# A hybrid decoder layer in split float32r on one Trainium2 core: the lower parts of some stationary weight pieces are summed by accumulating DMAs

## The chip, the cores and the metric

One core of one Trainium2 chip runs the whole layer as one program. The metric is device time in microseconds (us), the time of one execution. Three runs of the kernel before took 771.6, 767.98 and 767.42 us; their median is 767.98 us.

## The reference, cut to what matters

The layer has 512 tokens and a width of 1024. Three groups of heads read one normed input through one projection `w_in`, and one projection `w_out` merges them; then comes a SwiGLU feed-forward network of inner width 2816. Both parts are residual.

```python
h = rmsnorm(x, norm_mix); proj = h @ w_in
y_mla = mla_group(...)     # causal attention, low-rank q and kv
y_hg  = hgrn2_group(...)   # gated linear recurrence, chunkwise
y_mem = mem_group(...)     # cross-attention into 256 memory tokens
mix = concat([rmsnorm(y_mla), y_hg, rmsnorm(y_mem)])
x = x + mix @ w_out
h2 = rmsnorm(x, norm_ffn)
x = x + (silu(h2 @ w_gate) * (h2 @ w_up)) @ w_down
```

## The kernel before, in words

**Split products.** TensorE multiplies in fp32r, a float32 of fewer bits. Each operand is therefore cut in two: an upper part `hi`, which is the value cast to fp32r, and a lower part `lo = value - hi`. `mm3` (line 496) issues three matmuls for each product: hi by hi, hi by lo, lo by hi. For a weight that is the stationary operand the third of the three is the only one that reads the weight's `lo`.

**Weight pieces.** `load` (line 474) brings up to 1024 columns of a weight from HBM into a tile `wr` (3 buffers) with one DMA on SyncE's queue. `piece` (line 481) makes from up to 512 of its columns a pair: `wh`, cast by ScalarE (5 buffers), and `wl`, subtracted by VectorE (4 buffers). `pieces` (line 489) does this for a whole `wr` and hands out blocks of 128 columns. It is called in three places: `feat` (line 578), for the 20 blocks of `w_in` that come through `load` (40 pieces of 512 columns); the first eight of twelve row blocks of `w_out` (line 1132, 16 pieces); and `down` (line 1270), for `w_down`, where a block of six 128-wide steps gives a piece of 512 and one of 256 columns (24 times), and a block of four one piece of 512 (8 times). These are 112 pieces. All other weights (`wide`, the low-rank weights, the last rows of `w_out`, and gate and up in `fast`, line 1218) call `piece` directly.

**The order of the work.** Nothing is issued as it is written. A `Recorder` notes every operation with its tiles, and `run` (line 239) plays a list scheduler over them. It takes operations by priority, prices each (`price`, line 187), gives some operations to another engine where that ends sooner (a Copy activation with a scale may go from ScalarE to VectorE), keeps account of tile buffers, and writes out one fixed order for each engine. The engines then go through their own orders, and only semaphores hold them. So what TensorE does while it would wait for a piece is decided in the plan, not on the chip.

**The stages**, with the times of the profiled execution: the start (0 to 30 us) loads x and the first weights, splits x as it arrives, runs two products of `w_in` in turn (the accumulators `mm`), and sums the squares of x (tiles `td`, added up by VectorE), which four small matmuls with a column of ones (`tr<-ones,td`) turn into the norm of x. Then follow the recurrence and the low-rank products (to 200 us), attention, memory attention and the first eight rows of `w_out` as filler for TensorE (to about 345 us), the passage to the feed-forward network (to 440 us), and the network itself. Its products with gate and up are done by `fast`, one level of a Strassen-like scheme, on 384 columns at a time; between its steps the plan sets the `down` products of the stripe before. The last eight `down` products stand alone at the end.

Of the kernel before, what the change touches and what calls it, by code (L numbers as in the profile page):

```python
# [9 lines left out]
F32R = mybir.dt.float32r  # L10
I32 = mybir.dt.int32
U8 = mybir.dt.uint8
AF = mybir.ActivationFunctionType
ALU = mybir.AluOpType
# [3 lines left out]
S = 512  # L18
# [27 lines left out]
class Recorder:  # L46
# [140 lines left out]
    def price(self, o, outs, ins):  # L187
        n = max(self._free(a) for a in outs)
        if o.name == "dma_start":
            return 475  # L190
        if o.eng == "tensor":
            if o.name == "transpose":
                return 109
            if ins[0].dtype == F32R:
                return n / 2.4 + 12.5 if n >= 256 else max(1.67 * n, 107)
            return 222 if n <= 2 else 62 if n <= 32 else 118 if n <= 64 else 218 if n <= 128 else 1.7 * n
        m = max([self._free(a) for a in ins] + [n])
        fast = self.inside(ins)
        if o.eng == "scalar":
            fn = o.args[2] if o.name == "activation" else None  # L200
            if fn is not None:
                o.table = self.TABLES.get(str(fn).split(".")[-1])
            return (92 if fast else 45) + 0.835 * m + (190 if "accum_out" in o.kw else 0) + (100 if hasattr(o.kw.get("scale"), "ap") else 0)
        if o.eng == "vector":
            if o.name == "reciprocal":
                return 70 + 6.6 * m
            if o.name == "tensor_copy":
                return 66 + (0.55 if fast else 1.045) * m
            if o.name == "tensor_scalar":
                return 66 + (0.62 if fast else 1.045) * m + 60 * any(hasattr(a, "ap") for a in o.args[2:])  # L210
            if o.name == "memset":
                return 60 + 0.5 * m
            if o.name == "scalar_tensor_tensor":
                return 68 + 1.15 * m
            return 68 + 1.045 * m
        if o.name == "memset":
            return 40 + m * 0.8
        if o.name == "tensor_scalar":
            return 244 + 0.84 * m
        return 170 + 2.17 * m  # L220
# [18 lines left out]
    def run(self):  # L239
# [19 lines left out]
        table, dma, done, out, port = None, 0.0, 0, [], 0.0  # L259
        busy = {e: 0.0 for e in engs}  # L260
        while done < len(ops):
            best = None
            for e in engs:
                be = None
                for o in cand[e]:
                    t = max(free[e], o.ready)
                    if o.alts[e][5]:
                        t = max(t, port)
                    ok = True
                    if o.new:  # L270
                        need = {}
                        for k in o.new:
                            tag = self.tiles[k][0]
                            j = need.get(tag, 0)
                            free_ = slots[tag]
                            skip = 0
                            for q in order[tag]:
                                if q == k or skip >= len(free_):
                                    break
                                if q not in o.new:  # L280
                                    skip += 1
                            if len(free_) <= skip + j:
                                ok = False
                                break
                            t = max(t, sorted(free_)[skip + j])
                            need[tag] = j + 1
                    if not ok:
                        continue
                    t = max(t, free[e])
                    if len(o.alts) > 1:  # L290
                        fin = t + o.alts[e][3] + o.alts[e][4]
                        late = False
                        for e2 in o.alts:
                            if e2 != e:
                                t2 = max(free[e2], o.ready)
                                if o.alts[e2][5]:
                                    t2 = max(t2, port)
                                if e2 == o.home or t2 + o.alts[e2][3] + o.alts[e2][4] < fin:
                                    back = sum(q.alts[e2][3] for q in cand[e2] if q.prio < o.prio and q.home == e2 and q.ready <= t2 + 200)
                                    if t2 + back + o.alts[e2][3] + o.alts[e2][4] < fin:  # L300
                                        late = True
                        if late:
                            continue
                    c = (t, o.prio)
                    if t <= free[e] + 1e-9:
                        c = (free[e], o.prio)
                    if be is None or c < be[0]:
                        be = (c, o)
                if be is not None and (best is None or be[0][0] < best[0][0]):
                    best = be  # L310
                    beste = e
            assert best is not None, [(e, [(c.name, c.n, c.new) for c in cand[e][:3]]) for e in engs]
            (t, _), o = best
            for e in o.alts:
                cand[e].remove(o)
            o.eng = beste
            o.name, o.args, o.kw, cost, _, both = o.alts[beste]
            if o.eng != "scalar":
                o.table = None
            if o.table is not None and o.table != table:  # L320
                cost += 1300
                table = o.table
            end = t + cost
            if both:
                port = end
            free[o.eng] = end
            busy[o.eng] += cost
            if o.dma:
                ap = o.kw["out"]
                nb = self._free(ap) * ap.ap[0][1] * 4  # L330
                dma = max(dma, t + 1100) + nb / 360.0
                end = dma + 1500
            for k in o.new:
                tag = self.tiles[k][0]
                slots[tag].remove(min(slots[tag]))
                order[tag].remove(k)
            for k in o.tiles:
                last[k] = max(last[k], end)
                self.tiles[k][2] -= 1
                if self.tiles[k][2] == 0:  # L340
                    slots[self.tiles[k][0]].append(last[k] + 100)
            for s in o.succs:
                q = ops[s]
                q.left -= 1
                q.ready = max(q.ready, end + self.LAT.get((o.eng, q.eng), 0))
                if not q.left:
                    for e in q.alts:
                        cand[e].append(q)
            out.append((t, o))
            o.t, o.end = t, end  # L350
            done += 1
# [42 lines left out]
def body(ctx, tc, t):  # L394
    nc = tc.nc
    PS = bass.MemoryType.PSUM
    rec = Recorder(tc)
    V, A, G, T, DMA = rec.vector, rec.scalar, rec.gpsimd, rec.tensor, rec.sync
# [19 lines left out]
    def sb(tag, shape=(P, S), dt=F32):  # L418
        return rec.tile("SB", shape, dt, tag, nm(tag), BUFS[tag])
# [18 lines left out]
    def f(ap):  # L438
        return ap.bitcast(F32)
# [26 lines left out]
    def split(src, hi, lo, scale=None):  # L466
# [3 lines left out]
        else:  # L470
            A.activation(hi, src, AF.Copy, scale=scale)
            V.scalar_tensor_tensor(lo, src, scale, f(hi), ALU.mult, ALU.subtract)

    def load(src, n=1024):

        raw = sb("wr", (P, 1024))
        with rec.first(0):
            DMA.dma_start(out=raw[:, :n], in_=src)
        return raw

    def piece(raw, a, b):

        hi = sb("wh", dt=F32R)
        lo = sb("wl", dt=F32R)
        with rec.first(0):
            split(raw[:, a:b], hi[:, :b - a], lo[:, :b - a])
        return hi, lo

    def pieces(raw, n=1024):

        p = []
        for a in range(0, n, S):
            p.append(piece(raw, a, min(n, a + S)))
        return lambda k: cut(p[k // 4], slice(None), slice((k % 4) * P, (k % 4 + 1) * P))

    def mm3(out, l, r, first, last):
# [54 lines left out]
    with rec.first(0):  # L551
# [4 lines left out]
        for k in range(KD):  # L556
            if k in EARLY:
                n, tag = EARLY[k]
# [8 lines left out]
            hi = sb("xh", dt=F32R)  # L567
            lo = sb("xl", dt=F32R)
# [260 lines left out]
    with rec.first(0):  # L829
        for k in range(4):  # L830
            r = sb("td", (P, 2, NM))
            DMA.dma_start(out=r, in_=t["memT"][:, k * S:(k + 1) * S].rearrange("p (a b) -> p a b", a=2))
            hi = sb("mx", (P, 2, NM), F32R)
            lo = sb("mx", (P, 2, NM), F32R)
# [57 lines left out]
    for h in range(4):  # L892
        o = ps_mm()
# [10 lines left out]
    for b in range(NB):  # L904
        o = ps_mm()[:, :256]
# [3 lines left out]
        o = o.rearrange("p (h d) -> p h d", h=4)  # L909
# [44 lines left out]
    for i in range(2):  # L954
        w = [piece(r, i * S, (i + 1) * S) for r in wukv]
        for b in range(NB):
            o = ps_mm()
# [75 lines left out]
    for h in range(4):  # L1033
# [7 lines left out]
        o, qs = rope_t(qh, h)  # L1041
# [3 lines left out]
        o, kh2 = rope_t(kh, h)  # L1045
# [3 lines left out]
        for g in range(2):  # L1049
            pb = []  # L1050
            for b in (2 * g, 2 * g + 1):
# [3 lines left out]
                o = ps_at()  # L1055
# [32 lines left out]
    for h in range(4):  # L1088
        o = ps_mm()
# [18 lines left out]
    for h in range(4):  # L1108
# [6 lines left out]
        for g in range(2):  # L1115
            pb = []
            for b in (2 * g, 2 * g + 1):
                bs = slice(b * P, (b + 1) * P)
                o = ps_at()
# [287 lines left out]
```

## Time and profile before

| | before |
|---|---|
| median of the runs | 767.98 us |
| the profiled execution's own time | 769.33 us |
| its span, first to last instruction | 767.3 us |
| TensorE busy | 734.7 us (96%) |
| VectorE busy | 615.1 us (80%) |
| ScalarE busy | 391.6 us (51%) |
| GpSimd busy | 148.7 us (19%) |
| mean granted TensorE clock | 0.982 |
| DMA, mean over the span | 90 GB/s, queue of SyncE 29.4% of 16 engines |

PE is TensorE's matmuls and PEld its weight loads, DVE is VectorE, ACT ScalarE, POOL GpSimd, and SP SyncE, which here only issues DMAs. In a row, out<-in are the tiles with their shapes, x a count, then busy time in us and the mean of one in ns, then the idle time just before and what ended it. All recorded operations have the same line (370), so rows are told apart by tile names. A matmul's time is from its start to its end in the pipeline; the distance between starts is what TensorE spends on it.

### The profile page before, as it was taken

Reading aid. Unit: us, or ns where it says so; the run is one execution under the profiler, and the core shown is the slowest. Engines: PE = TensorE matmul, PEld = TensorE weight load, DVE = VectorE, ACT = ScalarE, POOL = GpSimd, SP = SyncE. Lnnn points to the kernel's source line nnn. Section 1 sums busy time; section 2 is a strip of 40 time slices with the busy share of each in tenths; the row PEclk is TensorE's granted clock in tenths of the full one; section 3 lists DMA queues with packets and bytes.
Section 4 is the critical chain, followed back from the end, with each engine's and each line's share of the span. In section 5 each row is a group of like instructions: output and inputs, shape, how many; then the busy total and the mean of one; then the engine's idle time right before and its main releaser. Section 6 shows DMA issues by size and latency. Waiting matters only on the chain.

```text
span 767.3 us, 12180 instructions
## 1 busy us (share of the span) xinstructions
PE 734.7 (96%) x4117; PEld 646.9 (84%) x4117; DVE 615.1 (80%) x1415; ACT 391.6 (51%) x790; POOL 148.7 (19%) x166
## 2 busy tenths in 40 slices
PE   6999998999999999899898799999999999999997
PEld 4899887888788888788677699999989998999986
DVE  6887788765997888896899899778887788886762
ACT  6543335226674476565475465455354553555440
POOL 1133233114201021010330203210221101201101
PEclk9999999899999999999999899999999999999999
DMA  8231113012541132211423423251522513142132
GB/s 274 71 111 47 65 56 96 21 28 87 163 136 56 51 128 83 69 43 54 146 62 95 124 82 93 73 156 40 145 83 84 154 41 107 56 123 71 35 110 97
DMA packets 36206, 69.38 MB, mean 90 GB/s; under 512 B 4272, under 2 KB 21296, under 8 KB 36144
## 3 DMA queue, kind: packets, MB, share of 16 engines
q1 hardware_dynamic: 36144, 68.61, 29.4%
q8 instruction: 32, 0.52, 0.3%
q14 instruction: 30, 0.25, 0.1%
HBM read 66.50 MB, written 2.10 MB: 89 GB/s over the span
## 4 chain that ended last, share of the span: by engine, by line
PE 64%; DVE 7%; issue 1%; DMA 1%; ACT 1%; DVEq 0%; ACTq 0%
PE mm L370 30%; PE tr L370 18%; PE at L370 17%; DVE wl L370 2%; DVE y L370 1%; DVE tm L370 1%; DVE p L370 1%; DMA mx<-in_wu 1%; DVE tc L370 1%; DVE mx L370 1%; DVE xl L370 0%; DVE hd L370 0%; DVE xh L370 0%; DVE sm L370 0%; DVE td L370 0%
## 5 line engine op out<-in xcount | busy, mean ns | idle before, releaser
L370 ACT CAST wh<-wr 128x512 fp32r<-128x512 f32 (+2 forms) x151 | 86.2, 575 | 120.6 <-PE mm L370 81.8
L370 ACT CAST wh<-mx 128x384 fp32r<-128x384 f32 (+1 forms) x160 | 77.5, 486 | 91.4 <-PE at L370 40.7
L370 PE MATMUL mm<-xh,wh 128*128 128x512 f32 x244 | 99.3, 410 | 7.1 <-ACT xh L370 7.1
L370 DVE TENSOR_TENSOR wl<-wr,wh 128x512 fp32r<-128x512 f32 (+2 forms) x141 | 96.7, 693 | 10.5 <-issue 4.0
L370 PE MATMUL mm<-xl,wh 128*128 128x512 f32 x244 | 99.4, 407 | 2.5 <-DVE xl L370 2.5
L370 PE MATMUL mm<-xh,wl 128*128 128x512 f32 x244 | 98.8, 405 | 0.0
L370 DVE TENSOR_TENSOR wl<-mx,wh 128x384 fp32r<-128x384 f32 (+1 forms) x141 | 74.1, 536 | 14.1 <-PE at L370 5.8
L370 PE MATMUL mm<-wh,hd 128*128 128x384 f32 (+2 forms) x232 | 71.2, 331 | 2.7 <-ACT wh L370 1.7
L370 PEld LDWEIGHTS mm<-xh,wh 128*128 128x128 f32 x244 | 46.9, 193 | 16.7 <-ACT xh L370 8.5
L370 PEld LDWEIGHTS mm<-xl,wh 128*128 128x128 f32 x244 | 46.9, 192 | 12.9 <-DVE xl L370 5.2
L370 PE MATMUL at<-wh,hd 128*128 128x384 f32 (+1 forms) x176 | 56.4, 325 | 0.0
L370 PEld LDWEIGHTS mm<-xh,wl 128*128 128x128 f32 x244 | 46.8, 192 | 8.6 <-DVE wl L370 0.4
L370 PE MATMUL tr<-xh,wl 128*128 128x512 f32 x132 | 52.0, 394 | 0.5 <-DVE wl L370 0.5
L370 PE MATMUL tr<-xl,wh 128*128 128x512 f32 x132 | 51.9, 393 | 0.0
L370 PE MATMUL tr<-xh,wh 128*128 128x512 f32 x132 | 51.7, 392 | 0.0
L370 ACT CAST wh<-y 128x384 fp32r<-128x384 f32 (+1 forms) x64 | 30.9, 486 | 35.4 <-PE at L370 19.5
L370 PE MATMUL mm<-wh,v 128*128 128x384 f32 (+1 forms) x128 | 42.5, 336 | 5.9 <-ACT wh L370 5.4
L370 PEld LDWEIGHTS mm<-wh,hd 128*128 128x128 f32 x232 | 43.0, 189 | 5.5 <-ACT wh L370 2.0
L370 DVE TENSOR_TENSOR tm<-tr,tm 128x512 f32<-128x512 f32 x30 | 20.6, 687 | 31.9 <-PE tr L370 31.9
L370 POOL TENSOR_TENSOR wl<-mx,wh 128x384 fp32r<-128x384 f32 (+1 forms) x19 | 19.3, 1016 | 129.4 <-PE at L370 51.6
L370 PE MATMUL at<-wh,v 128*128 128x384 f32 (+1 forms) x128 | 41.8, 330 | 0.0
L370 POOL TENSOR_TENSOR wl<-wr,wh 128x512 fp32r<-128x512 f32 (+2 forms) x17 | 21.4, 1264 | 104.6 <-PE mm L370 55.6
(369 smaller groups left out, 1968.8 us busy)
## 6 DMA issues: line engine op xcount, KB each, us to landing
wr<-in_wf SPq DMA_DIRECT2D x20, 512.0 KB, 3.4
wr<-in_wd SPq DMA_DIRECT2D x24, 384.0 KB, 3.2
mx<-in_wg SPq DMA_DIRECT2D x24, 192.0 KB, 2.7
y<-in_wg SPq DMA_DIRECT2D x24, 192.0 KB, 2.4
mx<-in_wu SPq DMA_DIRECT2D x24, 192.0 KB, 2.5
y<-in_wu SPq DMA_DIRECT2D x24, 192.0 KB, 2.6
tm<-in_xT SPq DMA_DIRECT2D x16, 256.0 KB, 4.1
wr<-in_wt SPq DMA_DIRECT2D x8, 512.0 KB, 4.2
```

Of the source, the lines that this page charges most:

```text
L370: r = getattr(getattr(self.nc, o.eng), o.name)(*[get(a) for a in o.args], **{k: get(a) for k, a in o.kw.items()})
```

## The change

The 112 pieces that `pieces` makes get their `lo` in another way. ScalarE casts `hi` as before; a second activation writes `-hi` into `lo`; then a DMA issued by GpSimd reads the same weights from HBM once more and adds them to `lo` in place. `load` notes for each `wr` where it came from. The scheduler's prices get an entry for such a DMA: 1000 ns of GpSimd to issue it instead of 475, and a transfer at 180 GB/s instead of 360. These are the plan's assumptions, not measurements.

```diff
-            return 475
+            return 475 if o.eng == "sync" else 1000
...
-                dma = max(dma, t + 1100) + nb / 360.0
+                dma = max(dma, t + 1100) + nb / (360.0 if o.eng == "sync" else 180.0)
...
+    def piece_dma(raw, a, b):
+        hi = sb("wh", dt=F32R)
+        lo = sb("wl", dt=F32R)
+        with rec.first(0):
+            A.copy(hi[:, :b - a], raw[:, a:b])
+            A.activation(lo[:, :b - a], f(hi)[:, :b - a], AF.Copy, scale=-1.0)
+            G.dma_start(out=lo[:, :b - a], in_=home[raw.tensor.name][:, a:b], accum_op=ALU.add)
+        return hi, lo
...
-            p.append(piece(raw, a, min(n, a + S)))
+            p.append(piece_dma(raw, a, min(n, a + S)))
```

Since the plan is made anew, the orders of all engines change. VectorE goes from 1413 to 1361 rows: 81 of its 110 subtractions from `wr` of 512 columns and all 25 of 256 columns are gone, 13 of the negations are given to it, and it takes over other operations. ScalarE goes from 758 to 832 rows and has 99 of the negations. GpSimd has 112 DMAs more and 25 tensor operations fewer.

At the start, TensorE's order around the four small matmuls `tr<-ones,td`. The accumulators mm_2157 and mm_2201 are the first two products of `w_in` in both orders, mm_2299 (before) and mm_2266 (after) the third; wl_2199 is the lower part of the second product's first piece. Before:

```order
L370 MATMUL mm_2299<-xl_2184,wh_2260 128x512
L370 MATMUL mm_2299<-xh_2176,wl_2276 128x512
L370 MATMUL mm_2299<-xh_2203,wh_2260 128x512
L370 MATMUL mm_2299<-xl_2213,wh_2260 128x512
L370 MATMUL mm_2299<-xh_2203,wl_2276 128x512
L370 MATMUL mm_2299<-xh_2216,wh_2266 128x512
L370 MATMUL tr_2328<-ones,td_2306 128x2 x4
L370 MATMUL mm_2299<-xl_2229,wh_2266 128x512
L370 MATMUL mm_2299<-xh_2216,wl_2288 128x512
```

After:

```order
L370 MATMUL mm_2157<-xl_2238,wh_2210 128x512
L370 MATMUL mm_2157<-xh_2229,wl_2217 128x512
L370 MATMUL mm_2157<-xh_2236,wh_2210 128x512
L370 MATMUL mm_2157<-xl_2244,wh_2210 128x512
L370 MATMUL mm_2157<-xh_2236,wl_2217 128x512
L370 MATMUL mm_2266<-xh_2149,wh_2256 128x512
L370 MATMUL mm_2266<-xl_2155,wh_2256 128x512
L370 MATMUL tr_2288<-ones,td_2275 128x2 x4
L370 MATMUL mm_2201<-xh_2149,wl_2199 128x512
L370 MATMUL mm_2201<-xh_2161,wh_2189 128x512
L370 MATMUL mm_2201<-xl_2172,wh_2189 128x512
```

Before the change 61 matmuls of 512 columns stand ahead of the small ones, after it 28; the second product, but for two matmuls, has moved behind them.

In the feed-forward network, TensorE's order where the third `down` product of the first stripe begins; tr_7663 (before) and tr_7730 (after) are its accumulator, wl_7645 and wl_7685 the lower part of its first piece, and mm and at are those of `fast`. Before:

```order
L370 MATMUL at_7619<-wh_7598,pth_6698 128x384
L370 MATMUL tr_7663<-xh_7275,wh_7613 128x512
L370 MATMUL tr_7663<-xl_7292,wh_7613 128x512
L370 MATMUL tr_7663<-xh_7275,wl_7645 128x512
L370 MATMUL tr_7663<-xh_7282,wh_7613 128x512
```

After:

```order
L370 MATMUL at_7680<-wh_7657,pth_6752 128x384
L370 MATMUL tr_7730<-xh_7331,wh_7674 128x512
L370 MATMUL tr_7730<-xl_7348,wh_7674 128x512
L370 MATMUL mm_7737<-wh_7706,v_6344 128x384
L370 MATMUL mm_7737<-wl_7719,v_6344 128x384
L370 MATMUL mm_7737<-wh_7706,v_6580 128x384
L370 MATMUL at_7742<-wh_7706,v_6344 128x384
L370 MATMUL at_7742<-wl_7719,v_6344 128x384
L370 MATMUL at_7742<-wh_7706,v_6580 128x384
L370 MATMUL mm_7737<-wh_7717,v_6344 128x384
L370 MATMUL at_7742<-wh_7717,v_6344 128x384
L370 MATMUL tr_7730<-xh_7331,wl_7685 128x512
```

Eight matmuls of `fast` now stand between the first use of the piece's upper part and the first use of its lower part.

At the same place GpSimd's order, where wl is the lower part of a weight piece, of gate and up if it comes from mx or y. Before:

```order
L370 TENSOR_TENSOR mx_7157<-y_7228,mx_7157 128x384
L370 TENSOR_TENSOR wl_7558<-mx_7112,wh_7550 128x384
L370 TENSOR_TENSOR wl_7609<-mx_7157,wh_7598 128x384
L370 TENSOR_TENSOR mx_7578<-mx_7578,mx_7571 128x384
L370 TENSOR_TENSOR wl_7787<-y_7215,wh_7755 128x384
```

After:

```order
L370 TENSOR_TENSOR wl_7661<-mx_7159,wh_7645 128x384
L370 TENSOR_TENSOR wl_7668<-mx_7213,wh_7657 128x384
L370 DMA wl_7685<-in_wd 128x512
L370 DMA wl_7702<-in_wd 128x256
L370 TENSOR_TENSOR mx_7687<-mx_7687,mx_7672 128x384
L370 TENSOR_TENSOR wl_7780<-y_7284,wh_7752 128x384
```

Each `down` product now puts two DMAs between GpSimd's subtractions for `fast`, and what stands behind them waits until they are issued.

More of the change, by code (lines that the diff above doesn't have):

```diff
@@ L472, in split @@
             V.scalar_tensor_tensor(lo, src, scale, f(hi), ALU.mult, ALU.subtract)
+    home = {}
     def load(src, n=1024):
@@ L478, in load @@
             DMA.dma_start(out=raw[:, :n], in_=src)
+        home[raw.tensor.name] = src
         return raw
```

## The prediction, as put on record before the run

> **What bounds the kernel now.** I read the page's busy times first, then the windows by stage, then what TensorE waited for.
>
> ```profile
> span 767.3 us, 12180 instructions
> ...
> PE 734.7 (96%) x4117; PEld 646.9 (84%) x4117; DVE 615.1 (80%) x1415; ACT 391.6 (51%) x790; POOL 148.7 (19%) x166
> ```
>
> TensorE is idle for 32.6 us of the span. That bounds what relief of VectorE can bring, apart from the clock. The windows, one row for each stage (busy us, granted clock, DMA share, GB/s), show where these 32.6 us lie:
>
> ```profile
> core 0: us, PE busy (x) PEld busy (x) DVE busy (x) ACT busy (x) POOL busy (x), PEclk, DMA share, GB/s
> 0.00:30.00 30.00, 23.87 (x100) 17.50 (x101) 21.21 (x51) 18.49 (x31) 2.92 (x8) 1.00 0.63 203
> 30.00:128.00 98.00, 97.38 (x670) 86.77 (x669) 78.73 (x202) 41.33 (x79) 32.35 (x47) 1.00 0.22 72
> 128.00:200.00 72.00, 67.67 (x373) 56.68 (x372) 52.07 (x141) 30.93 (x62) 23.75 (x25) 0.93 0.19 59
> 200.00:345.00 145.00, 143.02 (x789) 120.53 (x788) 127.06 (x353) 89.84 (x183) 17.75 (x22) 0.99 0.29 90
> 345.00:440.00 95.00, 81.72 (x389) 69.88 (x388) 83.44 (x178) 53.27 (x110) 18.91 (x15) 0.93 0.33 96
> 440.00:740.00 300.00, 298.02 (x1705) 276.82 (x1704) 244.43 (x485) 154.67 (x325) 49.15 (x47) 1.00 0.31 89
> 740.00:767.00 27.00, 23.02 (x102) 18.75 (x100) 8.12 (x12) 3.07 (x5) 3.88 (x3) 1.00 0.34 115
> ```
>
> Idle: 6.1 us at the start (before the first x is there), 0.6, 4.3, 2.0, 13.3, 2.0, and 4.0 at the end. In the feed-forward network, 300 us long, TensorE has nothing to gain: 2 us. The stages at 128 and 345 us have waits and also a clock of 0.93, which costs some 5.0 and 6.7 us more (7% of each). What ended TensorE's waits:
>
> ```profile
> PE mm L370 <- ACT wh L370: 7.1, 2, 5.4
> PE mm L370 <- ACT xh L370: 7.1, 2, 6.1
> PE mm L370 <- DVE xl L370: 2.5, 1, 2.5
> PE at L370 <- POOL tm L370: 1.9, 1, 1.9
> ...
> PE mm L370 <- DVE wl L370: 1.2, 3, 0.5
> ```
>
> The subtraction that the change takes away, DVE wl, is waited for by three matmul groups for 1.2 us in all. TensorE bounds the kernel, and the subtraction is hidden beside it.
>
> **VectorE, ScalarE and GpSimd.** The costs of one, by shape:
>
> ```profile
> L370 DVE TENSOR_TENSOR wl<-wr,wh 128x512 fp32r<-128x512 f32 x110 | 83.1, 757 | 8.7 <-issue 3.6 <-PE mm L370 2.7 <-PE tr L370 1.0
> L370 DVE TENSOR_TENSOR wl<-mx,wh 128x384 fp32r<-128x384 f32 x105 | 58.4, 567 | 10.4 <-PE at L370 5.1 <-PE tr L370 2.4 <-ACT wh L370 2.3
> ...
> L370 DVE TENSOR_TENSOR wl<-wr,wh 128x256 fp32r<-128x256 f32 x25 | 11.5, 459 | 1.6 <-PE at L370 0.7 <-issue 0.3 <-PE mm L370 0.3
> ...
> L370 DVE CAST wh<-wr 128x512 fp32r<-128x512 f32 x6 | 2.5, 424 | 0.9 <-PE mm L370 0.9
> ```
>
> ```profile
> L370 ACT CAST wh<-wr 128x512 fp32r<-128x512 f32 x117 | 72.3, 621 | 100.8 <-PE mm L370 68.0 <-PE tr L370 20.1 <-PE at L370 3.7
> ```
>
> VectorE loses 81 x 0.757 + 25 x 0.459 = 72.8 us, gains 13 negations at about 0.42 (the cast is the nearest row) = 5.5, and some 41 other operations (1413 - 106 + 13 = 1320, and it has 1361) at about 0.55 = 23: from 615 to about 570 us. ScalarE gains 77 negations at about 0.62 (the cast again) and 22 of half the width at less, 48 to 61 us, and hands some work on: about 430. Both stay below TensorE, so none of this is in the sum by itself. It counts only where VectorE holds TensorE: at 128 to 200 and at 345 to 440 us. In the second the order has no piece of the changed kind, and VectorE's 83.4 us there are the residual, its norm and the feed-forward operands, which stay: 0 us, with the bound below. In the first, TensorE's wait for POOL tm and its slow clock can go, because the plan sets 3.6 us more of matmuls ahead of that chain's last ones: between 0 and 4.3 + 5.0 = 9.3 us; I take 3, near the one wait of 1.9 with some clock.
>
> **The start.** Sums of squares and second product, before:
>
> ```profile
> 17.78 0.68 DVE L370 TENSOR_TENSOR td<-td,td 128x512 f32<-128x512 f32 x1
> 18.39 0.68 DVE L370 TENSOR_TENSOR wl<-wr,wh 128x512 fp32r<-128x512 f32 x1
> ...
> 22.60 0.68 DVE L370 TENSOR_TENSOR td<-td,td 128x512 f32<-128x512 f32 x1
> ...
> 22.86 0.39 PE L370 MATMUL mm<-xl,wh 128*128 128x512 f32 x1
> 23.09 0.39 PE L370 MATMUL mm<-xh,wl 128*128 128x512 f32 x1
> ...
> 23.55 0.95 PE L370 MATMUL tr<-ones,td 128*128 128x2 f32 x8
> ```
>
> Matmuls start 0.23 us apart, and the small ones come at 23.55, when td is ready. In the new order 28 instead of 61 wide matmuls stand ahead of them: 33 x 0.23 = 7.6 us of work has moved behind a point that TensorE cannot pass before td is ready. td comes sooner, though: between 17.78 and 23.28 VectorE does five adds and four subtractions at 0.6 us each; after, one negation and one cast (0.42 each) and the 0.42 mask cast stand there with four adds: 3.7 instead of 5.5 us, 1.8 sooner. ScalarE must then do its part by 20.6, and by its rows it can. TensorE starts the rest 7.6 - 1.8 = 5.8 us poorer, and in the 98 us that follow it is idle for 0.6 us, so nothing there gives this back: +5.8 us. This does not hang on the DMA's speed, since wl_2199, whose upper part is cast at 11 us, has some 10 us to land. If td came no sooner it would be 7.6; if ScalarE and VectorE ran free of it, 4.
>
> **The accumulating DMAs.** The profile has none, nor any DMA issued by GpSimd. The nearest row (KB each, us from issue to landing):
>
> ```profile
> wr<-in_wo SPq DMA_DIRECT2D x8, 256.0 KB, 2.7
> ```
>
> Below, a piece of 256 KB lands in 2.7 us, if adding costs nothing. Above, in twice that, if old and new data pass one after the other, and 1.0 us of GpSimd to write it out (as long as one of its tensor operations, below): 6.4. I take 4.5: 2.7, another 256 KB at the 321 GB/s that the start reaches (0.8), and 1.0 to issue, the estimates' middle.
>
> ```profile
> 10.00:20.00 10.00, 9.92 (x40) 7.03 (x40) 9.76 (x15) 8.98 (x16) 2.15 (x1) 1.00 0.89 321
> ```
>
> ```profile
> L370 POOL TENSOR_TENSOR wl<-mx,wh 128x384 fp32r<-128x384 f32 x15 | 16.3, 1090 | 102.0 <-PE at L370 48.1 <-ACT wh L370 41.8 <-ACT xh L370 6.2
> ```
>
> The chain for one piece: TensorE frees the buffer, ScalarE negates (0.62), GpSimd issues, the sum lands, TensorE reads. From td's end to the small matmuls a hand-over took 23.55 - 23.28 = 0.27 us; two such, 0.5, since the landing's is in its time. That is 0.5 + 0.6 + 4.5 = 5.6 us, with ends 3.8 and 7.5. Against it stands the room in TensorE's own order, from the last use of the buffer's piece before to the first use of the new one. Up to 345 us it is 5.6 us at the least and mostly 9 to 16: hidden, and at 7.5 us it costs 4. In the feed-forward network it is short. For wl_7685, whose buffer held wl_7635, 27 matmuls of 384 columns and two of 512 stand between:
>
> ```profile
> 475.65 0.33 PE L370 MATMUL at<-wl,hd 128*128 128x384 f32 x1
> 475.83 0.33 PE L370 MATMUL at<-wh,hd 128*128 128x384 f32 x1
> 476.00 0.33 PE L370 MATMUL mm<-wh,v 128*128 128x384 f32 x1
> ```
>
> 27 x 0.174 + 2 x 0.23 = 5.2 us. Counted so, the first pieces of the 24 `down` products among `fast` have 4.8 to 6.3 us but for one, about 5.6 in the mean; the second pieces, and the last eight products, have over 6.3 but for one. At a chain of 5.6 us the shorter half waits, 12 pieces for 0.1 to 0.8 us, in the mean 0.37: +4.5 us. At 5.1 it is nothing; at 6, +10; at 7.5, 24 x 1.9 = 46. Behind the issuing GpSimd stand subtractions for `fast`, 1.1 us each, for which matmuls wait in turn; ahead of it, ScalarE's casts for `fast` stand behind the negation. Subtractions for `fast` have less room too, since two of four wl buffers are held by a `down`: the tightest tenth of them 1.4 us instead of 2.4, against 0.57 for the subtraction and 0.54 for two hand-overs. The cover left is 0.3 us: 0 in the sum, and 0.3 us and more for each where VectorE comes late by that much. DMA time itself is no bound: 26 MB more beside the 0.31 share here.
>
> The Trainium skill speaks to this price. Collectives: The Full Stack, Part 3 (the bandwidth ceiling), says that a reducing DMA is half as fast as a copy since it needs two source reads; DMA: Bandwidth & Descriptors, Anatomy of one DMA, gives 2.0 us and bytes / 436 GB/s for a DMA from GpSimd. Its estimate for a plain 256 KB is 2.6 us, to which the 2.7 measured on SyncE's queue agrees; with double bytes 3.2 us, a chain of 4.3 and no wait at all. By that the sum would be 4.5 us less; no run here shows it yet.
>
> **The sum**, on the profiled execution: 769.3 + 5.8 - 3 + 4.5 = 776.6. That execution is 1.35 us above the median of the runs; on the median 768.0 + 7.3 = 775.
>
> **The rivals.** About 0.5% (3.8 us) is what a measurement here can tell from no change.
> - *Late landing.* The sum takes 6 us or more from issue, or GpSimd needs well over 1 us to write it out; the network's 24 `down` products then stall one by one, and GpSimd's subtractions with them. For: their room is so even that they all tip together, at a chain of 5.6 us. Against: the rows of plain loads. Price: 768 + 2.8 + 10 to 46 = 781 to 817, and TensorE's clock, which is 0.93 where it waits, could add to it.
> - *Early landing.* The sum lands within 4 us: no wait in the network, and the start and the chain at 128 us alone remain: 768 + 2.8 = 771, within 0.5%. The two pages of the Trainium skill named above would have it so.
> - *Faster: VectorE runs ahead.* Where VectorE is 88 to 93% busy (200 to 440 us), 48 pieces fewer let its chain into the network start sooner against TensorE, and the 13.3 us of waits and 6.7 us of clock at 345 to 440 shrink by half; those at 128 us go wholly. 768 + 5.8 - 9.3 - 10 = 755. It decides if more than 10 us of these 29 go and the sums land in time. Against: in TensorE's order the norm before the network stands 1.3 us later than before, not earlier, and the work between is what it was.
> - *It doesn't do what it says.* The plan fills VectorE up again, and everything stays as it was, start included: 768.
>
> **How the numbers follow.** Forecast (775, from 772 to 781) 0.40; late 0.22; early 0.20; faster 0.14; nothing 0.04. Faster by over 0.5%: 0.14. Within: early and nothing, 0.24. Slower: forecast and late, 0.62. The range leaves out the faster half of the one and the dearer half of the other: from 762 (half the gain) to 801 (+30 in the network, a chain of 6.9 us).
>
> **What would show it.** Right: VectorE near 570 and ScalarE near 430 us; the small matmuls at 21.8 us and TensorE idle for some 6 us between 12 and 22; in the issues, wl<-in_wf with landings near 4.5 us; waits of TensorE for wl from a DMA of a few us in all, between 440 and 740 us. Wrong: a landing of 6 us or more; GpSimd's issue over 1 us; the stage at 345 us with 8 us of idle or less; or TensorE as busy at the start as before.

## The result, and the profile after

The changed kernel took 791.71 us (median of 4 runs, 789.81 to 797.01), the kernel before 767.7 us beside it: a ratio of 1.0315, 95% interval 1.0281 to 1.035. It is 24 us slower; 7 were forecast. The profiled execution took 789.81 us. Its page, with busy times and DMA queues:

```profile
span 788.0 us, 12426 instructions
...
PE 736.3 (93%) x4117; PEld 642.4 (82%) x4117; DVE 572.3 (73%) x1363; ACT 423.8 (54%) x865; POOL 218.2 (28%) x253
...
q1 hardware_dynamic: 36144, 68.61, 28.8%
q0 software_dynamic: 16128, 26.22, 21.1%
```

The change does what it says: VectorE fell by 43 us, ScalarE rose by 32, and a second queue moves 26 MB, whose packets take 21.1% of the 16 DMA engines, nearly twice as much per byte as SyncE's 28.8% for 68.6 MB. TensorE is busy for nearly as long as before (736 us, 735 before), but it is idle for 51.7 us instead of 32.6. The same stages as before:

```profile
0.00:30.00 30.00, 21.53 (x68) 14.29 (x69) 18.06 (x53) 19.64 (x32) 5.79 (x13) 0.94 0.86 242
30.00:128.00 98.00, 97.85 (x668) 87.74 (x667) 71.06 (x188) 43.32 (x85) 32.26 (x47) 1.00 0.49 114
128.00:200.00 72.00, 68.61 (x407) 57.34 (x406) 53.70 (x152) 35.28 (x72) 26.53 (x29) 1.00 0.28 74
200.00:345.00 145.00, 142.19 (x802) 120.60 (x801) 119.67 (x349) 99.02 (x205) 37.70 (x45) 1.00 0.62 142
345.00:440.00 95.00, 82.94 (x398) 70.87 (x397) 86.15 (x180) 54.76 (x108) 21.88 (x18) 0.95 0.40 107
440.00:740.00 300.00, 281.86 (x1579) 257.62 (x1578) 208.34 (x419) 155.51 (x335) 82.12 (x89) 1.00 0.47 113
740.00:788.00 48.00, 41.33 (x205) 33.90 (x203) 15.32 (x30) 16.28 (x32) 11.92 (x14) 0.98 0.67 149
```

Two rows stand out. At the start TensorE has 68 matmuls done in 30 us where it had 100. Between 440 and 740 us it is idle for 18 us where it was for 2. Of the four stages between 30 and 440 us the first has two matmuls fewer than before and the others have more, and the granted clock at 128 to 200 is 1.00 instead of 0.93. TensorE's waits, and then those of its weight loads, which take in what matmuls still in the pipeline hide:

```profile
PE tr L370 <- DMA wl<-in_wd: 16.1, 19, 2.4
PE mm L370 <- ACT wh L370: 7.1, 2, 5.0
PE mm L370 <- ACT xh L370: 6.2, 2, 5.5
PE tr L370 <- DVE td L370: 2.8, 2, 2.1
```

```profile
PEld tr L370 <- DMA wl<-in_wd: 22.3, 22, 2.8
```

The row of the sums is new: 22 times the weight load of a `down` product waits for its sum, 22.3 us in all, 1.0 us each.

Where on the way the time is lost shows best when the two traces are laid over each other by matmuls. The table gives how much later (+) or sooner (-) than in the kernel before the n-th matmul starts, counted from the first; it is worked out from the matmuls' start times in the traces. The orders differ, so the n-th matmul is not always the same product; both kernels have 4117. In the kernel before, matmul 1100 starts at about 190 us, 2000 at 358, 2400 at 455.

| n-th matmul | 100 | 1100 | 2000 | 2400 | last (4117) |
|---|---|---|---|---|---|
| changed kernel, us | +6.8 | +0.4 | -0.9 | -3.4 | +21.6 |

The start costs 6.8 us, the middle gives 10.2 back, and the network takes 25.0. Together that is 21.6 us where the medians differ by 24: the profiled execution is the fastest of the four, and that of the kernel before took 1.6 us more than its median.

### The profile page after: what moved, and what is told of

The parts are those of the page before. It is cut to its first block, busy times and chain, and to the rows that moved or that the text cites. A ratio compares the mean times of both kernels' runs of the same rounds, so it can differ in the third digit from the quotient of the medians.

```text
span 788.0 us, 12426 instructions
## 1 busy us (share of the span) xinstructions
PE 736.3 (93%) x4117; PEld 642.4 (82%) x4117; DVE 572.3 (73%) x1363; ACT 423.8 (54%) x865; POOL 218.2 (28%) x253
## 3 DMA queue, kind: packets, MB, share of 16 engines
q1 hardware_dynamic: 36144, 68.61, 28.8%
q0 software_dynamic: 16128, 26.22, 21.1%
## 4 chain that ended last, share of the span: by engine, by line
PE 44%; DMA 16%; DVE 6%; issue 4%; ACT 3%; POOL 1%; ACTq 0%; DVEq 0%; POOLq 0%
PE mm L370 19%; PE tr L370 16%; DMA wl<-in_wd 14%; PE at L370 9%; DVE wl L370 2%; ACT wl L370 1%; DVE mx L370 1%; ACT wh L370 1%; DMA wl<-in_wo 1%; DMA wl<-in_wf 1%; POOL wl L370 1%; DVE xl L370 1%; DMA mx<-in_wu 0%; DVE tc L370 0%; DVE tm L370 0%
## 5 line engine op out<-in xcount | busy, mean ns | idle before, releaser
L370 ACT CAST wh<-wr 128x512 fp32r<-128x512 f32 (+2 forms) x145 | 83.1, 577 | 113.6 <-PE mm L370 70.7
L370 ACT CAST wh<-mx 128x384 fp32r<-128x384 f32 (+1 forms) x155 | 75.0, 486 | 93.8 <-PE tr L370 46.3
L370 DVE TENSOR_TENSOR wl<-mx,wh 128x384 fp32r<-128x384 f32 (+1 forms) x131 | 70.2, 545 | 19.0 <-PE at L370 7.1
L370 POOL DMA_DIRECT2D wl<-in_wd x56 | 49.8, 950 | 73.9 <-ACT wl L370 56.3
L370 PE MATMUL tr<-xh,wl 128*128 128x512 f32 x132 | 53.9, 409 | 15.4 <-DMA wl<-in_wd 15.3
L370 ACT ACTIVATE wl<-wh 128x512 fp32r<-128x512 f32 (+1 forms) x99 | 56.8, 580 | 16.8 <-issue 5.7
L370 POOL DMA_DIRECT2D wl<-in_wf x40 | 35.2, 881 | 95.1 <-ACT wl L370 54.4
L370 POOL TENSOR_TENSOR wl<-mx,wh 128x384 fp32r<-128x384 f32 (+1 forms) x29 | 27.7, 956 | 110.6 <-PE tr L370 33.4
L370 PE MATMUL tr<-xh,wh 128*128 128x512 f32 x132 | 51.7, 391 | 0.0
```

What stands on the lines that cost most here:

```text
L370: r = getattr(getattr(self.nc, o.eng), o.name)(*[get(a) for a in o.args], **{k: get(a) for k, a in o.kw.items()})
```

## The experiments

The theory was that the loss is TensorE's wait for sums that land late in the network (the landing theory). Its rivals were a cost spread over all pieces (GpSimd's issue, ScalarE's negations, HBM traffic) and a shortage of wl buffers. Each row is one of the edits below; each ratio is to the kernel before on the same chip, with its 95% interval. Delays are as in the table above.

| kernel | median us | ratio | n=100 | 1100 | 2000 | 2400 | last |
|---|---|---|---|---|---|---|---|
| `down` subtracted | 766.99 | 1.0004 (0.9981 to 1.0028) | +6.3 | +0.9 | -0.5 | -2.9 | -2.9 |
| only `down` accumulated | 789.56 | 1.0301 (1.026 to 1.0341) | +1.5 | +1.4 | +1.4 | +0.3 | +20.9 |
| late plan | 772.85 | 1.0073 (1.0045 to 1.0101) | +7.0 | +0.2 | -3.2 | -7.7 | +4.3 |
| plain copy | 766.54 | 0.9979 (0.9955 to 1.0003) | +8.6 | +3.4 | -0.4 | -2.4 | +2.8 |
| five wl buffers | 786.39 | 1.0248 (1.0203 to 1.0293) | +6.6 | +1.6 | -1.1 | -4.2 | +17.3 |
| start subtracted | 783.41 | 1.0193 (1.0161 to 1.0226) | +0.8 | -4.5 | -6.4 | -8.4 | +16.6 |
| start and `down` subtracted, late plan | 757.17 | 0.9861 (0.9834 to 0.9888) | +1.3 | -2.5 | -5.9 | -10.2 | -10.3 |
| start subtracted, late plan | 767.36 | 1.0012 (0.9987 to 1.0038) | +0.5 | -2.2 | -5.5 | -9.6 | -1.0 |
| start and `down` subtracted | 759.73 | 0.991 (0.9878 to 0.9942) | +0.4 | -5.1 | -6.6 | -9.5 | -9.4 |
| start subtracted, late plan, five buffers | 767.4 | 1.0003 (0.9974 to 1.0032) | +1.2 | -2.9 | -4.5 | -9.3 | -1.9 |
| start and `down` subtracted, late plan, five buffers | 758.85 | 0.9897 (0.9846 to 0.9948) | +0.6 | -4.9 | -6.5 | -10.1 | -9.4 |

### Half of the pieces each

`pieces` takes the way of cutting as an argument; `down` hands in `piece`, the others keep `piece_dma`.

```diff
-            p.append(piece_dma(raw, a, min(n, a + S)))
+            p.append((cut_ or piece_dma)(raw, a, min(n, a + S)))
...
-        w = pieces(load(t["wd"][i][:, j0 * P:(j0 + n) * P], n * P), n * P)
+        w = pieces(load(t["wd"][i][:, j0 * P:(j0 + n) * P], n * P), n * P, piece)
```

> The 56 pieces of the down products are subtracted by VectorE again; the 56 others keep the accumulating DMAs. Landing theory (the loss is the wait of TensorE for late sums in the feed-forward network): the 25 us lost after 440 us go, and what stands at 440 us stays, 3 us ahead of the kernel before: 763 to 767 us. Rival (GpSimd's issue time, ScalarE's negations and the added HBM traffic cost everywhere): half of the pieces, so about half of the 24 us stays, near 779 us.

766.99 us, at the upper edge of what the landing theory gave and 12 us from the rival. In the network nothing is lost any more. Its window:

```profile
440.00:740.00 300.00, 297.62 (x1699) 276.32 (x1698) 244.26 (x481) 152.28 (x319) 49.72 (x47) 1.00 0.30 90
```

TensorE is idle for 2.4 us of the 300, as before the change (2.0). The other way round, `pieces` subtracts and only `down` accumulates:

> Only the 56 pieces of the down products are accumulated by DMA; all others are subtracted. Landing theory: the start and the middle are as before, and the network loses its 25 us: 790 to 795 us. Rival (cost spread over all pieces): about 780 us.

789.56 us, just under the 790 to 795 expected: most of the loss (20.6 us after matmul 2400, where the changed kernel lost 25.0) with half of the DMAs and 44% of their bytes. The waits:

```profile
PE tr L370 <- DMA wl<-in_wd: 13.0, 16, 1.5
PE mm L370 <- DVE wl L370: 3.6, 7, 0.9
```

The cost is not spread over the pieces; it sits in the `down` products. The start is not late in this kernel, and the middle gains 1.2 us where the changed kernel gains 10.2: both come from the other 56 pieces.

### A plan that reckons with the later landing

```diff
-                end = dma + 1500
+                end = dma + (1500 if o.eng == "sync" else 2800)
```

> All 112 pieces by DMA, but the plan reckons with a landing that is 1.3 us later (5.4 us from issue instead of 4.1 for 256 KB). Landing theory, in the form that TensorE's fixed order leaves too little room: the waits for wl from a DMA in the network fall from 22 us to under 8, and the time to 770 to 780 us. Rival (four wl buffers cannot hold sums that are on their way for so long, whatever the order): the waits move to the products with gate and up, as waits for their subtractions, and the time stays at 785 to 795 us.

772.85 us, and the waits for sums in the network fell to

```profile
PE mm L370 <- DVE wl L370: 4.1, 7, 1.1
PE tr L370 <- DMA wl<-in_wd: 2.9, 3, 2.0
```

(4.8 us by the weight loads, from 22.3). The same 112 DMAs in another order lose 19 us less: most of the loss was a fixed order that looked for the sums too soon. The rival has a part: 12 us are still lost between matmul 2400 and the last, and waits for subtractions rose from 2.7 to 4.1 us.

### The same order, a copy in place of the sum

The DMAs copy the weight over the negated part, so that the lower part is the whole weight and what is computed is something else; orders and bytes from HBM are the same.

```diff
-            G.dma_start(out=lo[:, :b - a], in_=home[raw.tensor.name][:, a:b], accum_op=ALU.add)
+            G.dma_start(out=lo[:, :b - a], in_=home[raw.tensor.name][:, a:b])
```

> The same order, but GpSimd's 112 DMAs copy instead of adding, so the lower part is the whole weight and the products are other numbers. If the addition makes the landing late: the landing of 256 KB falls from 5.0 to under 4 us and the waits in the network from 22 to under 5 us, time near 771 us. If GpSimd's queue makes it late: the landing stays over 4.5 us and the time over 783 us.

766.54 us, below the 771 expected. (The profiled execution took 770.97, the most of this kernel's eight, and the delays in the table are from it.) GpSimd's queue by packets, MB and share, and then the landings, in this kernel:

```profile
q0 software_dynamic: 16128, 26.22, 12.5%
```

```profile
wl<-in_wf POOLq DMA_DIRECT2D x40, 256.0 KB, 3.5
...
wl<-in_wd POOLq DMA_DIRECT2D x32, 256.0 KB, 3.9
```

and in the changed kernel:

```profile
wl<-in_wf POOLq DMA_DIRECT2D x40, 256.0 KB, 4.7
...
wl<-in_wd POOLq DMA_DIRECT2D x32, 256.0 KB, 5.1
...
wl<-in_wd POOLq DMA_DIRECT2D x24, 128.0 KB, 5.3
```

Adding makes the landing 1.2 us later, and with 3.9 us, which is under the 4.1 that the plan reckons with, TensorE waits for sums for

```profile
PE tr L370 <- DMA wl<-in_wd: 1.4, 3, 0.8
```

The same packets take 21.1 / 12.5 = 1.7 times as long when they add. GpSimd writes out a plain DMA in 0.57 us and an adding one in 0.88 (means of the `w_in` pieces; 0.55 and 0.95 for `down`), which is a part of the 1.2. Between matmul 2400 and the last this execution still loses 5.2 us.

### One more buffer

Five wl buffers; eight instead of twelve tiny tiles pay for the space.

```diff
-        "wr": 3, "wh": 5, "wl": 4, ... "sm": 12, ...
+        "wr": 3, "wh": 5, "wl": 5, ... "sm": 8, ...
```

> As changed, with five wl buffers instead of four (and eight instead of twelve of the tiny tiles sm, to make room). TensorE's order then leaves the accumulated pieces in the network 5.6 us at the tightest tenth and 7.2 in the median, instead of 5.1 and 6.6. If the chain of 6.4 us against this room is the whole loss: 0.4 to 0.5 us less wait for most of the 24 products, 8 to 12 us, so 780 to 784 us. If the loss is that of the DMA queue or of GpSimd, more buffers change nothing: 789 to 793 us.

786.39 us: a gain of 5 instead of the 8 to 12 that I expected, between the two theories, and hardly clear of noise (the two ratios' intervals overlap). The waits of TensorE for the sums hardly fell:

```profile
PE tr L370 <- DMA wl<-in_wd: 14.8, 16, 2.4
```

Matching the built order with the records of the 56 `down` pieces tells why. The negation now starts 0.96 us after its buffer is free, not 0.30, so the buffer no longer holds it; but from the DMA's issue to the first matmul that reads the sum there are 6.42 us in the mean as there were 6.40. For the first pieces of the 24 products, on which TensorE waits, it is 5.0 and 5.3, and with the wait taken off 4.2 and 4.4: no more room than before. The plan, which reckons with a landing after 4.1 us, uses the fifth buffer to put the reading sooner as well, not to give the sum time. My count of room from the buffer's last use was right in number only because in the plan with four buffers the two ends meet.

### The start

The first two weights that come through `load` are subtracted.

```diff
+    early_w = [piece, piece]
...
-            w = pieces(raw)
+            w = pieces(raw, 1024, early_w.pop() if early_w else None)
```

> As changed, but the first two weights that come through load are subtracted, so that 59 wide matmuls stand ahead of the small ones at the start, as 61 did before and 28 did after. The 6.8 us that the hundredth matmul comes late fall under 1.5. If a late start is carried to the end: 784 to 787 us. If it is paid back from waits that TensorE has anyway at 128 to 200 us: no change, 789 to 793 us.

783.41 us, 8 us less by the medians, and the hundredth matmul is 0.8 us late instead of 6.8. The start's window has as many matmuls as before the change (x99, x100):

```profile
0.00:30.00 30.00, 24.32 (x99) 18.74 (x100) 20.47 (x52) 19.45 (x32) 4.81 (x10) 1.00 0.72 221
```

Most of the late start is carried to the end: this kernel starts 6.0 us better, and at matmul 2400 and at the last it stands 5.0 us ahead of the changed one. Its middle gives 9.2 us where that of the changed kernel gave 10.2, so 1 us was repayment and the rest is a gain of its own.

### Together

With both losses taken out, and the late plan for what still accumulates:

> The first two weights and the down products are subtracted, and the plan reckons with a landing 1.3 us later for the accumulated rest. If what VectorE's relief gives in the middle is real and comes on top of a full start: 6 to 10 us under the kernel before, 757 to 761 us. If the start's loss and the middle's gain are the same waits: 763 to 767 us.

757.17 us, 1.4% under the kernel before (interval 1.1 to 1.7%); the gain of the middle stands. It is carried through the network without loss:

```profile
345.00:440.00 95.00, 84.15 (x415) 73.80 (x414) 86.99 (x182) 56.87 (x111) 19.58 (x16) 0.95 0.37 105
440.00:740.00 300.00, 298.10 (x1690) 274.96 (x1689) 239.38 (x470) 148.66 (x311) 52.83 (x49) 1.00 0.32 93
```

With `down` accumulated again:

> As changed, with the first two weights subtracted and a plan that reckons with the later landing; the down products stay with accumulating DMAs. From 772.9 us with the late plan alone: 766 to 768 if a late start is carried, 771 to 774 if it is paid back anyway. More than 780 would say that the late plan's gain hung on the start.

767.36 us: 5.5 under the late plan alone, so the late start is carried here too. Without the late plan:

> The first two weights and the down products are subtracted; the plan reckons with the landing that the change gave it. The kernel with the late plan as well took 757.2 us. If fewer subtractions on VectorE bring the gain in the middle, and the late plan only keeps TensorE from waiting for landings that here have 9 us and more of room: 757 to 761 us. If the late plan itself made a better order: 763 to 767 us.

759.73 us. The intervals of this ratio and of the 757.17 kernel's overlap, so the late plan can't be told to matter where the sums have room. With a fifth buffer, first with `down` accumulated and then subtracted:

> All but the first two weights accumulated, late plan, five wl buffers. From 767.4 us with four: the 9 us that its network still loses are waits for subtractions (4.6 us for DVE wl) and for sums (3.2 us). If four buffers are what makes these: 759 to 763 us. If it is GpSimd's and ScalarE's added work: 766 to 769 us.

> The first two weights and the down products subtracted, late plan, five wl buffers. The sums of the rest have room enough, so a fifth buffer should bring little beside 757.2 us: 755 to 759 us. Under 754 would say that buffers bind the middle as well.

767.4 and 758.85 us: the same as with four. Buffers are not what the network's last 7 to 9 us hang on. What TensorE waits for there, with `down` accumulated, the late plan and five buffers, is no longer the sums but VectorE's subtractions, for which it waited 0.8 us in the network of the kernel before:

```profile
PE mm L370 <- DVE wl L370: 4.4, 5, 1.1
```

Why these come late is open. The rival that is left, the added work on GpSimd and ScalarE, was expected at 766 to 769 and fits, but no run took that work away by itself, and the order that the plan made is another possible cause.

## Why the prediction was right and wrong

**What bounds the kernel: right in the main.** TensorE bounds it; that the subtractions are wholly hidden fits less well with the gain of the middle, below. VectorE came to 572 us (about 570 forecast), ScalarE to 424 (430).

**The start: right, its size in part by luck.** +5.8 us forecast, +6.8 measured. The mechanism is the one given: the small matmuls come when td is ready,

```profile
20.59 1.05 PE L370 MATMUL tr<-ones,td 128*128 128x2 f32 x8 [2.15 <-DVE td L370]
```

with TensorE idle ahead of them and 33 wide matmuls behind them, and subtracting the first two weights undid it. But td came 3.0 us sooner and not 1.8 (20.6 us, 21.8 forecast), so the sum's own terms give 7.6 - 3.0 = 4.6, and TensorE was idle for 2.3 us between 12 and 22, not for some 6. What made up for it was not in the sum: behind the wait the granted clock was low,

```profile
21.00:25.20 4.20, 4.20 (x15) 3.42 (x16) 2.11 (x13) 0.00 (x0) 0.00 (x0) 0.59 0.94 212
```

and the wide matmuls started 0.43 us apart instead of 0.23, which cost eight of them 1.6 us. The last 0.6 us are the count from the first matmul, which starts that much sooner than before.

**The middle: right in sign, too small.** -3 us were taken of 0 to 9.3 at 128 to 200 us, and 0 at 345 to 440. Measured: 6.4 us up to matmul 1100, where waits and the slow clock of 128 to 200 us went, then 1.3 up to matmul 2000, and 2.5 from there to 2400 (358 to 455 us before the change), together 10.2. The step "0 us, with the bound below" failed, and the waits that I took a third of went by two thirds. With 52 pieces accumulated and the two losses taken out, 7 to 10 us of this are a gain over the kernel before. It comes with the accumulated pieces of `w_in` and `w_out`: every kernel that has them gains 9 us or more between matmuls 100 and 2400, and the one that accumulates only `down` gains 1.2. That fewer subtractions on VectorE are the cause fits this, but is argued; whether the new orders have a part of it by themselves was not tried.

**The network: the step that failed.** It is the landing, "I take 4.5", and with it the chain, "0.5 + 0.6 + 4.5 = 5.6 us". One `down` piece in the trace of the changed kernel, ScalarE, GpSimd and TensorE, and the landing of this DMA, 5.4 us from its issue:

```profile
476.37 0.63 ACT L370 ACTIVATE wl<-wh 128x512 fp32r<-128x512 f32 x1
...
477.37 0.88 POOL L370 DMA_DIRECT2D wl<-in_wd  x1
...
482.80 0.50 PE L370 MATMUL tr<-xh,wl 128*128 128x512 f32 x1 [1.20 <-DMA wl<-in_wd]
```

```profile
wl<-in_wd POOLq DMA_DIRECT2D x1, 256.0 KB, 5.4
```

From the negation's start to the matmul 6.43 us, and the matmul starts as soon as the sum has landed. In the terms of the sum, as means over the first pieces of the 24 products: 0.35 from the freed buffer to the negation, 0.63 for the negation, 0.34 to GpSimd, 5.1 for the landing instead of 4.5, and 0.1 to the matmul, together 6.6 instead of 5.6. The landing is 0.6 of this 1 us; the hand-overs are the rest. The room was as counted: 6.6 less the wait of 0.9 us at the weight loads is 5.7. At a chain over all of these rooms every microsecond is paid 24 times, and 24 x 0.9 = 22 us is what the weight loads waited for sums (22.3). The other 3 of the 25.0 us are not accounted for in full; waits of the weight loads for VectorE's subtractions rose there from 2.1 to 3.4 us. So the forecast's own scale (nothing at a chain of 5.1, +10 at 6, +46 at 7.5) held; its place on that scale was wrong.

The time and the mechanism, 24 products that tip together, are those of the rival called late landing (781 to 817 us), to which I gave 0.22, and not of the likeliest case. But its condition, 6 us or more from the issue or well over 1 us of GpSimd, did not come true: 5.1 and 0.95 were enough. TensorE's clock added nothing in the network, where it stayed at 1.00.

The landing was mis-sized in both of its halves. A plain DMA from GpSimd lands after 3.9 us in the network, where I had 2.7 of SyncE's queue and 1.0 for the issue, 3.7; and the addition costs 1.2 us, where I had 0.8. By an estimate from two pages of the Trainium skill it would be 3.2 us (DMA: Bandwidth & Descriptors, Anatomy of one DMA, with twice the bytes as Collectives: The Full Stack, Part 3, has it for the reducing step of a collective), and this case's 4.7 to 5.1 do not agree. The rule there that an addition halves the rate fares better: the packets took 1.7 times as long.

**The other rivals.** Early landing fell with the sums; the plain copy, which lands after 3.9 us, bears out its condition, since the network then hardly waits for them. Faster by VectorE's relief (755 us) put 19.3 us on the stages at 128 and 345 us, and 10.2 came, 2.5 of them behind 358 us; a version with start and network left out took 757, but the price of 755 had the late start in it. GpSimd's subtractions behind its DMAs made no wait of TensorE that the profile names.

## What to carry to other kernels

Where a planner fixes an order on every engine, an assumed latency is a promise: its consumers are set close behind it, so here a landing 1 us later than assumed (5.1 for 4.1) was paid by nearly every one of 24 of them, and telling the plan of 1.3 us more took most of that away. Before moving work off an engine that is not the bound, look at where the moved result has room: the same DMAs made TensorE wait only twice, for 2.2 us, where mostly 9 us and more lay between buffer and use, and cost 1 us each where 5.6 lay. A term that multiplies a guess by 24 deserves the wide end of its range, not its middle.

## What the runs showed of the hardware

A DMA issued by GpSimd that adds 256 KB from HBM to SBUF landed 4.7 us (pieces of `w_in`) to 5.1 us (`down`) after its issue began, in the median, and a plain copy of the same bytes 3.5 to 3.9. GpSimd was busy 0.88 us (`w_in`) to 0.95 us (`down`) with writing out the first and 0.57 to 0.55 us with the second. The addition's packets held the DMA engines 1.7 times as long. A piece of half the size, issued right behind one of full size on the same queue, landed no sooner (5.3 us). At 128 to 200 us the granted clock, 0.93 before, was 1.00 where TensorE's wait of 1.9 us for GpSimd was gone, and 0.93 in the kernel that accumulates only `down`, which has that wait. At the start a wait of 2.15 us was followed by 4.2 us at a granted clock of 0.59, but the longest wait in the network, 2.4 us, by 1.00 over as long; so the length of one wait does not decide it. Behind the first came 1 us of small matmuls (two columns each), behind the second wide ones; whether that makes the difference is open.
